# A raw tile for the plain piece and tiles for the unsummed blocks in the first ff's up, in place of a context row and two dot tiles

## The chip, the cores and the metric

The kernel runs on one core of a Trainium2 chip. The metric is the device time of one execution in microseconds (us). The kernel before takes 2824.02 us, the median of 3 runs (2817.88 to 2826.64). The profile is one further execution on the same kind of chip.

## The reference

One layer of a diffusion backbone works on 256 latent tokens and 256 context tokens, 2048 wide, in float32. What matters here:

```
m    = silu(c) @ w_ada + b_ada            # latent: 9 chunks of 2048 (shift, scale, gate for three sub-layers)
m_c  = silu(c_ctx) @ w_ada + b_ada        # context: the same map
h    = rms_norm(s) * (1 + scale) + shift
s    = s + 0.5 * gate * ((silu(h @ w_gate) * (h @ w_up)) @ w_down)     # first ff, 5632 hidden, latent and context
...  token mixing (attention and a long convolution), then a second ff on the latent tokens alone
```

The context is needed only until the mixing's keys and values, so of its modulation only chunks 0 to 4 are used; the latent stream needs all nine.

## The kernel before

Each product is made of three matmuls: a float32 operand is split into a rounded part (`hi`, tile `whi`, a cast on ACT) and a remainder (`lo`, tile `wlo`, a subtraction on DVE), and `mm3` (lines 239 to 241) multiplies hi by hi, hi by lo and lo by hi.

The first ff's up runs over 44 blocks of hidden units, `f1.up(j)`. The first three (`WAVE`) run together in an opening wave. For each later block the 2048 inputs come in four pieces `kq`, each a weight load of 512 KB into a tile `raw` by `weight_load` (line 216, on SP's queue):

- piece 0 is the *plain* one. `prepare` casts it on ACT (L417), negates the cast (L418), and POOL adds the raw weights to it by an accumulating transfer (`u<-raw`, L419). The raw tile is free when the second of these transfers has read it. Piece 0 of block j+1 is prepared after piece 1 of block j.
- pieces 1 to 3 are *summed* from block 9, 7 and 5 on (`QUADS`): a scheme in the manner of Strassen with 14 products of 256 columns in place of 16. `prepare` first splits three of the four 128-wide blocks of the raw tile as they are (the *unsummed* blocks, 128x768: cast L208, subtraction L209), then forms sums in place on DVE (L425, L426, L427), and splits all four (128x1024, L208 and L209 again).

`raw` has four tiles; `whi` and `wlo` have three each, taken in turn by the short and the long splits. After block j PE's banks are combined (L469 to L477) on ACT and DVE, and `keep` (L483 to L487) writes the result to DRAM from ACT and POOL. The summed inputs themselves are made on DVE in the first blocks (`build`).

Beside this, DVE computes modulation chunks 5, 7, 6, 8 (`ADA_UP`) during the up and 2, 3, 4 (`ADA_DOWN`) during the down as dot products: `ada_dve` loads a half row of the transposed map (512 KB, tile `adaw`, four tiles) and multiplies it with a row of silu(c) (`crow0`) and, for chunks below 5, one of silu(c_ctx) (`crow1`), 1.28 us each (L145). `ada_hook` gives out dots after each piece at a rate (`ADA_RATES`: up, and the two passes of the down); `last_load` puts each dot's load behind the weight load traced last on SP's queue. Both rows and the dot tiles lie in the pool `adap`, which is opened after the wave and closed after the down; the rows are loaded by ACT's queue after block 3.

The down (`f1.down`) reads the activations back (POOL, L502) and takes 80 steps of one weight tile each (`weight`: cast L228, subtraction L232) with a call of the hook at each.

A planner orders the instructions of each engine and queue from the program's order and its own estimate of when tiles are free and transfers have landed. At run time every engine and queue goes through its list in that order and waits where something is not there.

## Time and profile before

| what | us |
|---|---|
| median of 3 runs | 2824.02 |
| the profiled execution, its own time | 2818.97 |
| its span, first to last instruction | 2817.2 |
| up with summed pieces, 260 to 1197 | 937.0, PE busy 819.2 |
| down with the dots, 1197 to 1670 | 473.0, PE busy 462.5 |
| the rest, 1670 to 2817 | 1147.0, PE busy 1136.2 |

Times in the profile count from the span's start. A line of a group reads: source line, engine, operation, out<-in by tile name, shapes, count | busy us, mean ns of one | idle time of the engine just before, and what ended it. A line of waits reads: engine, tile and line that waited <- what it waited for: us in total, times, the longest. "PEld" is the weight load of TensorE, "SPq" the DMA queue of SyncE. A busy PE is not PE at its peak, since matmuls overlap and the clock granted to it varies (PEclk, 1.00 is full).

### The profile page before, as it was taken

What the parts mean: (1) busy time and instruction counts of PE and PEld (TensorE: products, weight loads), DVE (VectorE), ACT (ScalarE), POOL (GpSimd) and SP (SyncE); (2) the same over time, 40 slices, a digit from 0 to 9 for tenths busy, and PEclk for the clock granted to TensorE, in tenths of its full rate; (3) what the DMA queues carried; (4) which work ended last, traced back from release to release, by engine and by line L of the source; (5) the groups of instructions that cost most, each with busy time, mean ns of one, the idle gap of its engine ahead of it and who ended that gap; (6) DMA issues with size and microseconds to landing.
All of it is one profiled execution on the core that took longest, in us unless ns stands there. A gap on an engine that the chain in (4) does not pass through costs nothing.

```text
span 2817.2 us, 38140 instructions
## 1 busy us (share of the span) xinstructions
PE 2662.6 (95%) x14480; PEld 2275.9 (81%) x14480; DVE 1910.3 (68%) x3050; ACT 1116.5 (40%) x1545; POOL 253.5 (9%) x394
## 2 busy tenths in 40 slices
PE   8999998988888889899999999999999999999999
PEld 5677888887888878787888798888878888888887
DVE  6756776766776676776898879688875455554444
ACT  5343443434333433321121145546554444444333
POOL 1121111111111111232001100000000000000000
PEclk9999999999999999899999999999999999999999
DMA  9977676767766676899679755634555666666664
GB/s 365 352 232 212 183 214 196 221 196 199 196 200 198 190 209 189 252 393 319 237 261 300 268 189 176 187 112 134 179 170 189 188 191 190 188 191 204 201 202 157
DMA packets 194004, 607.91 MB, mean 216 GB/s; under 512 B 22299, under 2 KB 25308, under 8 KB 189468
## 3 DMA queue, kind: packets, MB, share of 16 engines
q1 hardware_dynamic: 140012, 501.77, 53.7%
q0 software_dynamic: 53184, 100.95, 14.9%
q10 hardware_dynamic: 624, 2.75, 0.3%
q8 instruction: 113, 1.85, 0.3%
q14 instruction: 71, 0.58, 0.1%
HBM read 545.08 MB, written 38.81 MB: 207 GB/s over the span
## 4 chain that ended last, share of the span: by engine, by line
PE 59%; issue 19%; DMA 12%; DVE 6%; POOL 2%; ACT 2%; SPq 0%; POOLq 0%; DVEq 0%; ACTq 0%
PE pa L1254 10%; PE pa L1252 10%; PE pa L1253 9%; DMA adaw<-in_w_adaT_dram 5%; DMA u<-raw 4%; PE pb L241 4%; PE pb L239 4%; PE pb L240 4%; PE pa L247 3%; PE pa L241 3%; PE pa L239 3%; PE pa L240 3%; PE pa L249 2%; DVE adas L145 1%; DMA act<-u 1%
## 5 line engine op out<-in xcount | busy, mean ns | idle before, releaser
L232 DVE TENSOR_TENSOR wlo<-raw,whi 128x1024 fp32r<-128x1024 f32 x487 | 595.5, 1223 | 413.3 <-ACT whi L228 411.5
L228 ACT CAST whi<-raw 128x1024 fp32r<-128x1024 f32 x487 | 512.3, 1052 | 891.6 <-PE pa L1254 413.4
L241 PE MATMUL pa<-u,wlo 128*128 128x256 f32 (+1 forms) x1252 | 416.0, 332 | 36.0 <-DVE wlo L209 29.4
L241 PE MATMUL pb<-u,wlo 128*128 128x256 f32 (+1 forms) x1262 | 412.9, 328 | 37.5 <-DVE wlo L209 30.6
L239 PE MATMUL pa<-u,whi 128*128 128x256 f32 (+1 forms) x1252 | 415.1, 332 | 31.1 <-ACT whi L208 29.0
L239 PE MATMUL pb<-u,whi 128*128 128x256 f32 (+1 forms) x1262 | 412.0, 327 | 25.7 <-ACT whi L208 25.7
L1252 PE MATMUL pa<-whi,u 128*128 128x512 f32 x1060 | 413.9, 391 | 0.0
L1253 PE MATMUL pa<-wlo,u 128*128 128x512 f32 x1060 | 412.8, 390 | 0.2 <-DVE wlo L232 0.2
L1254 PE MATMUL pa<-whi,u 128*128 128x512 f32 x1060 | 412.8, 390 | 0.0
L240 PE MATMUL pa<-u,whi 128*128 128x256 f32 (+1 forms) x1252 | 410.9, 328 | 0.4 <-DVE u L789 0.4
L240 PE MATMUL pb<-u,whi 128*128 128x256 f32 (+1 forms) x1262 | 408.4, 324 | 0.0
L208 ACT CAST whi<-raw 128x768 fp32r<-128x768 f32 x222 | 205.4, 938 | 300.0 <-DVE raw L427 253.1
L145 DVE CUSTOM_DVE_ANT_0 adas<-adaw,crow,mod 128x1024 bf16<-128x1024 f32 x160 | 205.4, 1284 | 162.8 <-DMA adaw<-in_w_adaT_dram 160.8
L209 DVE TENSOR_TENSOR wlo<-raw,whi 128x768 fp32r<-128x768 f32 x222 | 240.2, 1089 | 107.9 <-ACT whi L208 106.9
L241 PEld LDWEIGHTS pb<-u,wlo 128*128 128x128 f32 x1262 | 249.7, 198 | 61.8 <-DVE wlo L209 37.5
L241 PEld LDWEIGHTS pa<-u,wlo 128*128 128x128 f32 x1252 | 249.7, 199 | 61.7 <-DVE wlo L209 35.7
L239 PEld LDWEIGHTS pa<-u,whi 128*128 128x128 f32 x1252 | 249.2, 199 | 57.7 <-ACT whi L208 32.3
L239 PEld LDWEIGHTS pb<-u,whi 128*128 128x128 f32 x1262 | 249.4, 198 | 47.5 <-ACT whi L208 29.2
L145 DVE CUSTOM_DVE_ANT_0 adas<-adaw,crow,cond 128x1024 bf16<-128x1024 f32 x160 | 205.3, 1283 | 112.2 <-DMA adaw<-in_w_adaT_dram 106.0
L240 PEld LDWEIGHTS pa<-u,whi 128*128 128x128 f32 x1252 | 249.3, 199 | 18.5 <-DVE u L789 1.5
L240 PEld LDWEIGHTS pb<-u,whi 128*128 128x128 f32 x1262 | 249.4, 198 | 16.8 <-issue 0.4
L1253 PEld LDWEIGHTS pa<-wlo,u 128*128 128x128 f32 x1060 | 199.1, 188 | 41.5 <-DVE wlo L232 0.6
(337 smaller groups left out, 3652.6 us busy)
## 6 DMA issues: line engine op xcount, KB each, us to landing
adaw<-in_w_adaT_dram SPq DMA_DIRECT2D x223, 512.0 KB, 6.4
raw<-in_w_dn_dram SPq DMA_DIRECT2D x184, 512.0 KB, 3.8
raw<-in_w_up_dram SPq DMA_DIRECT2D x176, 512.0 KB, 3.5
raw<-in_w_up1q_dram SPq DMA_DIRECT2D x164, 512.0 KB, 4.5
u<-act POOLq DMA_DIRECT2D x136, 256.0 KB, 9.0
act<-u POOLq DMA_DIRECT2D x132, 256.0 KB, 2.6
wrow<-in_w_ada_dram SPq DMA_DIRECT2D x32, 1024.0 KB, 9.9
u<-raw POOLq DMA_DIRECT2D x82, 256.0 KB, 6.3
```

The source lines that it names most:

```text
L145: V.tensor_tensor_reduce(out=sc, in0=t, in1=crow[i][:, b * (D // 2) : (b + 1) * (D // 2)], scale=1.0, scalar=mcol if b else bada[:, n : n ...
L208: S.copy(hi, src)
L209: V.tensor_sub(lo, src, hi.bitcast(F32))
L228: S.copy(hi, raw)
L232: V.tensor_sub(lo, raw, hi.bitcast(F32))
L239: PE.matmul(ps, w[0], xx[0], start=start, stop=False)
L240: PE.matmul(ps, w[0], xx[1], start=False, stop=False)
L241: return PE.matmul(ps, w[1], xx[0], start=False, stop=stop)
L247: PE.matmul(ps, w[0], x, start=start, stop=stop)
L1252: PE.matmul(ps[t], hi, w[0], start=start, stop=False)
L1253: PE.matmul(ps[t], hi, w[1], start=False, stop=False)
L1254: last = PE.matmul(ps[t], lo, w[0], start=False, stop=stop)
```

## The change

In the up, `adap` holds one context row (`crow0`) and two dot tiles. The 16 KB per partition given up there hold one raw tile for the plain piece (`plain`, 4 KB; from block 4 on, that is all but the first one prepared) and two tiles each for the rounded and the remainder part of the unsummed blocks (`bhi`, `blo`, 3 KB each). The four `raw` tiles are left to pieces 1 to 3, and the three `whi` and `wlo` to the long splits and to the pieces that aren't summed. The row is loaded ahead of block 3.

After the up the remaining dots of `ADA_UP` are run, `adap` is closed and opened again with both rows, loaded and put through Silu anew, and four dot tiles. The hook starts with a debt of 4, and the rates in the down are 1.15 and 1.42 in place of 1.05 and 1.4.

```
-ADA_RATES = (0.79, 1.05, 1.4)
+ADA_RATES = (0.79, 1.15, 1.42)
 ...
-        t = T(adap, (P, D // 2), "adaw", bufs=4)
+        t = T(adap, (P, D // 2), "adaw", bufs=adaw_bufs)
 ...
-    def weight_load(src, shape, queue=None):
-        raw = T(wp, shape, "raw", bufs=4)
+    def weight_load(src, shape, queue=None, pool=None):
+        raw = T(wp, shape, "raw", bufs=4) if pool is None else T(pool, shape, "plain", bufs=1)
 ...
-            raw = weight_load(self.wupq[j - WAVE, kq], (P, 2, 4, P))
+            pool = adap if kq == 0 and j > WAVE else None
+            raw = weight_load(self.wupq[j - WAVE, kq], (P, 2, 4, P), pool=pool)
 ...
-                hi, lo = T(wp, (P, 2, n, P), "whi", F32R, 3), T(wp, (P, 2, n, P), "wlo", F32R, 3)
+                if n == 3:
+                    hi, lo = (T(adap, (P, 2, n, P), name, F32R, 2) for name in ("bhi", "blo"))
+                else:
+                    hi, lo = (T(wp, (P, 2, n, P), name, F32R, 3) for name in ("whi", "wlo"))
                 out.append(split_to(raw[:, :, 0:n], hi, lo))
 ...
-    adap_cm = tc.tile_pool(name="adap", bufs=2)
-    adap = adap_cm.__enter__()
     crow = []
+
+    def open_dots(n, bufs):
+        nonlocal adap, adap_cm, adaw_bufs
+        adap_cm = tc.tile_pool(name="adap", bufs=2)
+        adap, adaw_bufs = adap_cm.__enter__(), bufs
+        crow.clear()
+        for i in range(n):
+            crow.append(T(adap, (P, D), f"crow{i}", bufs=1))
+            nc.scalar.dma_start(crow[i], a["crow"][i : i + 1, :].partition_broadcast(P))
+            S.activation(crow[i], crow[i], AF.Silu)
+
+    adap = adap_cm = adaw_bufs = None
+    open_dots(1, 2)
 ...
         f1.up(j)
         if j == WAVE:
-            for i in range(2):
-                crow.append(T(adap, (P, D), f"crow{i}", bufs=1))
-                nc.scalar.dma_start(crow[i], a["crow"][i : i + 1, :].partition_broadcast(P))
-                S.activation(crow[i], crow[i], AF.Silu)
             f1.hook = lambda: (next(build, None), ada_hook())
 ...
     norm_plan = iter(NORM_PLAN)
+    while done[0] < len(ADA_UP) * KT * 2:
+        ada_next()
+    adap_cm.__exit__(None, None, None)
+    open_dots(2, 4)
+    owed[0] = -4.0
+
     def down_hook(p):
```

## The prediction

> **What bounds the kernel now.** I read the page first, then the busy times by stage, the waits of the widest gap, and last one stretch of that stage in order of time.
>
> ```profile
> span 2817.2 us, 38140 instructions
> PE 2662.6 (95%) x14480; PEld 2275.9 (81%) x14480; DVE 1910.3 (68%) x3050; ACT 1116.5 (40%) x1545; POOL 253.5 (9%) x394
> ```
>
> PE leaves some 155 us of the span open. The view of windows (PE, weight loads, DVE, ACT, POOL, granted clock, DMA share, GB/s) says where:
>
> ```profile
> core 0: us, PE busy (x) PEld busy (x) DVE busy (x) ACT busy (x) POOL busy (x), PEclk, DMA share, GB/s
> 150.00:260.00 110.00, 105.97 (x503) 88.82 (x502) 64.72 (x112) 47.03 (x70) 21.95 (x30) 0.98 0.80 224
> 260.00:1197.00 937.00, 819.18 (x5470) 763.65 (x5469) 664.01 (x1094) 361.04 (x519) 146.15 (x199) 0.94 0.71 204
> 1197.00:1670.00 473.00, 462.51 (x2120) 383.58 (x2119) 369.45 (x584) 99.79 (x101) 65.44 (x123) 1.00 0.84 287
> 1670.00:2817.00 1147.00, 1136.20 (x5447) 949.25 (x5445) 708.21 (x1015) 542.91 (x736) 0.00 (x0) 1.00 0.57 178
> 843.40:847.20 3.80, 3.04 (x15) 2.84 (x15) 3.48 (x5) 1.07 (x3) 1.77 (x2) 0.56 0.91 115
> 847.40:853.40 6.00, 6.00 (x52) 6.00 (x52) 3.72 (x5) 2.74 (x4) 0.00 (x0) 1.00 0.63 147
> ```
>
> 118 of the 155 us lie in 260 to 1197, the first ff's up with its summed pieces; and there the clock is 0.94, because it is low after each stop (0.56 with 15 matmuls in 3.8 us, then 1.00 with 52 in 6.0). All the rest of the kernel is PE-bound. One hidden block j of that stage takes 25.33 us, by the first and last Silu of 39 ((1198.5 - 235.9) / 38), so the window holds 37 of them:
>
> ```profile
> L476 ACT ACTIVATE sq<-sq x39: 622/632/636, 235.9 to 1198.5; 128x512 f32<-128x512 f32 x39
> ```
>
> What PE would need: three summed pieces of 14 products with 3 matmuls each are 126 matmuls of 256 columns, at 6.0 / 52 = 0.115 us; the plain piece has 24 of 512 columns, at 200 / 901 = 0.222 us by this row of the later ff:
>
> ```profile
> 2150.00:2350.00 200.00, 200.00 (x901) 165.50 (x900) 101.21 (x99) 85.88 (x100) 0.00 (x0) 1.00 0.61 190
> ```
>
> That is 14.5 + 5.3 = 19.8 us, 733 us for 37. So the window could be 204 us shorter if only PE counted. The waits inside the window say who holds it up:
>
> ```profile
> DVE adas L145 <- DMA adaw<-in_w_adaT_dram: 161.9, 59, 6.0
> DVE wlo L209 <- ACT whi L208: 101.1, 90, 2.3
> ...
> PE pb L241 <- DVE wlo L209: 30.6, 25, 4.1
> PE pa L241 <- DVE wlo L209: 29.4, 29, 3.1
> ...
> PE pa L239 <- ACT whi L208: 29.0, 14, 3.2
> ...
> PE pb L239 <- ACT whi L208: 25.7, 17, 3.1
> ```
>
> PE's 118 us are waits for rounded and remainder tiles (114.7 in these four rows). Behind them stands DVE: 664.0 busy + 161.9 for dot tiles + 101.1 for ACT = 927 of 937 us. DVE works through its queue in order and is never idle for want of PE; **DVE's queue is the bound of this stage**, though busy only 71%.
>
> Why the dot tiles are late stands in SP's own waits, and in one block's stretch:
>
> ```profile
> SPq L216 <- DVE wlo L209: 424.7, 58, 11.0
> SPq L216 <- DMA u<-raw: 270.4, 38, 10.5
> ```
> ```profile
> 860.79 9.75 SPq L216 DMA_DIRECT2D raw<-in_w_up1q_dram  x2
> 870.58 0.44 SPq L141 DMA_DIRECT2D adaw<-in_w_adaT_dram  x1
> 879.92 0.80 SPq L216 DMA_DIRECT2D raw<-in_w_up1q_dram  x2
> 880.78 0.90 SPq L141 DMA_DIRECT2D adaw<-in_w_adaT_dram  x2
> ```
> ```profile
> 870.19 1.22 POOL L419 DMA_DIRECT2D u<-raw  x1
> ```
> ```profile
> DMA to landing us min/median/max: 3.3/6.3/9.7
> ```
> ```profile
> 873.99 2.27 DVE L209 TENSOR_TENSOR wlo<-raw,whi 128x1024 fp32r<-128x1024 f32 x2 [1.17 <-ACT whi L208]
> 879.44 1.28 DVE L145 CUSTOM_DVE_ANT_0 adas<-adaw,crow,mod 128x1024 bf16<-128x1024 f32 x1 [3.18 <-DMA adaw<-in_w_adaT_dram]
> ```
>
> Of four raw tiles one is the plain piece's. It is free only when POOL's second accumulating transfer has read it: issued at 870.19, landed 9.7 us later at 879.9 (the maximum of that line's landings), and SP's next raw load leaves at 879.92. That is once per block: 38 waits, 7.1 us each. The raw tile it holds back is a summed piece's, and the dot tiles queue behind it. The dot at 879.44 has its tile from 870.58, 8.9 us earlier.
>
> **The change, part by part.** The sum is made on DVE's 937 us.
>
> *The plain piece's own raw tile, and four raw tiles for three summed pieces.* No summed piece waits for the accumulating transfer any more; it waits for DVE's work four pieces back, more than a block. Of the 59 dot waits I lay 38 to SP's 38 stops, at the mean of 161.9 / 59 = 2.74 us: 104 us. The other 21, 58 us, follow loads that no stop delayed: they are a tile's time to land against where the dot stands in DVE's order, and stay. Bounds for the 104: all gone, or all kept, since the plain load now waits for the same transfer (one tile, last block's accumulation), on SP, with a dot tile and the next raw load queued behind it, and DVE and ACT behind those. One of about three dot tiles per block is traced right behind the plain load, so something remains: I take 20 us, nearer the lower end, since the next raw pieces are then already there and DVE has work to do first. Saved: 84 us.
>
> *Own rounded and remainder tiles (two each) for the three-block part.* The short cast no longer takes turns with the long one in three tiles. DVE's groups in the window:
>
> ```profile
> L209 DVE TENSOR_TENSOR wlo<-raw,whi 128x1024 fp32r<-128x1024 f32 x109 | 133.4, 1223 | 84.9 <-ACT whi L208 84.9
> L209 DVE TENSOR_TENSOR wlo<-raw,whi 128x768 fp32r<-128x768 f32 x108 | 103.2, 955 | 17.2 <-ACT whi L208 16.2
> L145 DVE CUSTOM_DVE_ANT_0 adas<-adaw,crow,mod 128x1024 bf16<-128x1024 f32 x60 | 77.0, 1283 | 84.8 <-DMA adaw<-in_w_adaT_dram 84.6
> ...
> L145 DVE DVE_READ_ACCUMULATOR2_ANT mod<- 128x1 f32 x120 | 10.1, 84 | 0.0
> ```
>
> The 16.2 us before the short subtraction go: they are a cast that was late for a tile or a load. The 84.9 before the long one stay: in-place subtractions, then ACT's cast, then DVE, in series whatever the tiles. Bounds: 0 to 101 saved, the upper if the next piece's short subtraction fills the gap, which the new tiles permit; I take 16. PE also gets more pieces in hand, which helps only if DVE keeps up on the mean.
>
> *Two dot tiles instead of four in the up.* SP's load of a dot now waits for the dot two before it, with the next raw load behind it. 120 dots in 937 us are 7.8 us apart, so a load has 15.6 us:
>
> ```profile
> DMA to landing us min/median/max: 4.4/6.7/11.1
> ```
>
> Even the longest landing of a dot tile fits: nothing. If dots ran in close threes, the third would wait up to 6.7 us; 0 to 20 us in all.
>
> *One context row fewer in the up, loaded before the up.* Dots there use one row. Gone: a broadcast of 1 MB and a Silu of 1.9 us on ACT; the other load keeps its place in ACT's queue at the wave's end. Nothing to -2; I take -2.
>
> ```profile
> u<-act POOLq DMA_DIRECT2D x136, 256.0 KB, 9.0
> ...
> crow<-in_crow_dram ACTq DMA_DIRECT2D x2, 1024.0 KB, 4.5
> ```
> ```profile
> L897 ACT ACTIVATE crow<-crow x2: 1902/1904/1905, 157.2 to 161.5; 128x2048 f32<-128x2048 f32 x2
> ```
>
> *Pool closed and opened again at the down.* The two dots that 160 steps of 0.79 leave (126 of 128) run at the up's end. Then ACT has two loads, which wait for the old tiles' last readers, and two Silus; behind these stand the casts of the down's weights, and PE behind those. Loads of 4.5 to 9.0 us (the latter what transfers take when the down's activations stream in) and 3.8 us of Silu make 12.8 to 21.8 us. Cover for the dots: the debt of 4 means that at 1.15 per step the first comes with the fifth step, and a step is 24 x 0.222 = 5.3 us, so 26.6 us. Cover for PE: the casts run ahead,
>
> ```profile
> ACT whi L228 <- PE pa L240: 186.1, 48, 6.7
> ```
>
> they wait for PE to free one of three tiles, so about two steps, 10.7 us, are in hand. Without all overlap the cost is 21.8 - 10.7 = 11 us; I take 3. Denser dots: 1.42 x 2 x (1.283 + 0.084) + 1.223 = 5.1 us of DVE per step, 5.3 of PE: still covered; before it was 1.4.
>
> The Trainium skill's page "DMA: Bandwidth & Descriptors", section "Queues, rings and completion order", says that each DMA engine takes turns between the queues with work, packet by packet. By that rule the two context rows would share the engines with the weights and the activations and, at a third of the 287 GB/s of the row 1197 to 1670, take some 22 us (an estimate); with the Silus 26 us, the cost 26 - 10.7 = 15 in place of 3, and the total 2737. No row of before shows that load in such traffic.
>
> Sum: DVE's window becomes 937 - 84 - 16 = 837 us, above PE's 733, so DVE stays the bound. With -2 and +3 the change is -99. The profiled execution's own time is 2818.97 us (span 2817.2, 1.8 around it), so 2720; the median of the runs lies 5.05 above that execution. **Forecast: 2725 us.**
>
> **The rivals.**
> *PE becomes the bound:* all dot waits and half of ACT's go, DVE needs 664 + 50 + 10 = 724, less than PE's 733. With a few stops left, 770: gain 167, 2657 us. For it: deeper tiles let DVE fill gaps. Against: in-order DVE at 724 of 733 leaves no slack.
> *It does not do what it says:* SP keeps its order, plain load ahead of the next summed piece, so these still leave when the accumulation lands. The 270 us of SP stops remain, only the 16.2 and a few waits of PE go: gain 10 to 45, about 2795. For it: the stops are SP's, and the plain load's source of delay, 3.3 to 9.7 us, is untouched. Against: four tiles let the summed load go earlier.
> *Slower:* the stop moves onto the plain load, and the dot tile behind it becomes the late one. Before, plain load and its dot tile left at 870.2 and 870.58, freed by DVE; now they would leave at 879.9, 9.7 us later, the tile landing at about 880.3 + 6.7 = 887.0 instead of 879.4. If DVE's order keeps the dot where it stands, each block pays 7.6 and saves 2.74: +4.9 x 37 = +180, near 3000. It decides when DVE reaches that dot less than 4.9 us later in its work than now; half way it is +90, 2914.
>
> **How the numbers follow.** Forecast with its neighbourhood (gain 45 to 150): 0.56. PE bound: 0.13. Little done: 0.14, most of it still over 0.3% faster (0.3% is about what can be told from no change here, 8 us). Slower: 0.13. No change: 0.04. The range, 2665 to 2815, holds the forecast, the little-done case and the upper part of PE bound: 0.8 together. Its ends are gains of 159 (just short of where PE binds) and of 10 (only the late short casts gone, less the down's cost). Faster 0.81, same 0.06, slower 0.13.
>
> **What would show it.** In 260 us to the up's end: about 22.6 us between Silus; DVE's waits for dot tiles from 161.9 down to about 80 with fewer than 40 stops; the long subtraction still waiting some 85 on ACT; SP's waits for the accumulation now before plain loads alone; clock up from 0.94. Wrong if DVE's waits for dot tiles stay above 140, if PE's busy share in the stage passes 97%, or if the down's first 100 us grow by over 15.

## The result and the profile after

The changed kernel takes 2807.73 us (median of 7 runs, 2801.81 to 2812.43) against 2823.61 us (7 runs, 2816.01 to 2826.64): a ratio of 0.995 with a 95% interval of 0.9934 to 0.9965. It is some 16 us faster; the forecast was 99. The profiled execution took 2812.43 us, the longest of its seven, 6.5 us less than the one before; the traces can account for these 6.5 us only.

The page of the changed kernel, its span and its first engine line:

```profile
span 2810.7 us, 37981 instructions
PE 2653.9 (94%) x14480; PEld 2255.6 (80%) x14480; DVE 1914.2 (68%) x3050; ACT 1112.7 (40%) x1546; POOL 253.5 (9%) x394
```

Where the 6.5 us come from is read from three lines of code. The copy of a bank by ACT (L469 before, L473 after) runs once in each block of the first ff's up, so its last start is the up's end; the first matmul of the projection to keys and values (L965, L982) is the down's end. Each row gives count, shortest, median and longest duration in ns, first and last start. Before:

```profile
L469 ACT COPY sq<-pb x20: 362/374/377, 226.4 to 1194.0; 128x256 f32<-128x256 f32 x20
L965 PE MATMUL pa<-whi,u x128: 387/389/628, 1690.7 to 1927.1; 128*128 128x512 f32 x128
```

After, with the Silu of the blocks (L480):

```profile
L473 ACT COPY sq<-pb x20: 358/363/374, 236.5 to 1163.8; 128x256 f32<-128x256 f32 x20
L480 ACT ACTIVATE sq<-sq x39: 620/631/634, 242.6 to 1166.6; 128x512 f32<-128x512 f32 x39
L982 PE MATMUL pa<-whi,u x128: 387/389/629, 1682.8 to 1919.2; 128*128 128x512 f32 x128
```

The up ends 30.2 us earlier (1163.8 against 1194.0). The stretch from there to the projection grows by 22.3 us, from 496.7 to 519.0. A block takes 24.32 us ((1166.6 - 242.6) / 38) in place of 25.33; the prediction expected 22.6.

Of the 30.2 us, 10.7 come in the last block alone. PE begins its products at 1162.39 before and at 1142.88 after, 19.5 us earlier:

```profile
1162.39 0.40 PE L239 MATMUL pb<-u,u 128*128 128x512 f32 x1
```
```profile
1142.88 0.40 PE L239 MATMUL pb<-u,u 128*128 128x512 f32 x1
```

So this block takes 31.6 us to its bank copy before and 20.9 us after. Before, seven dot instructions (L145) start between the last two bank copies and 132 by the up's end; in the changed kernel none and 128, since the next dots wait for the second opening. A part of what the up gains there is work that comes later.

**The up.** The waits in 260 to 1197 (total, times, longest, in us). The window is that of the prediction and here includes 33 us of the down, so its totals are, if anything, a little high for the up:

```profile
DVE adas L145 <- DMA adaw<-in_w_adaT_dram: 156.5, 51, 7.9
...
DVE wlo L209 <- ACT whi L208: 65.6, 60, 1.2
...
PE pa L239 <- ACT whi L208: 21.5, 15, 5.7
PE pa L241 <- DVE wlo L209: 20.6, 21, 2.3
...
PE pb L239 <- ACT whi L208: 17.1, 13, 4.3
...
PE pb L241 <- DVE wlo L209: 14.5, 20, 1.4
...
DVE blo L209 <- ACT bhi L208: 13.6, 14, 2.6
```

PE's waits in these rows fell from 114.7 to 73.7 us, and DVE's waits for ACT from 101.1 to 79.2 (65.6 + 13.6). Its waits for dot tiles, from which 84 us were to come, are 156.5 against 161.9. SP's own waits in the same window show that its stops did not go, they changed place:

```profile
SPq L216 <- DVE wlo L209: 399.3, 81, 9.9
SPq L216 <- DMA u<-plain: 157.2, 36, 8.2
SPq L141 <- DMA adaw<-in_w_adaT_dram: 139.7, 41, 5.8
```

The stop on the accumulation is now at the plain piece's own load (`u<-plain`, 36 times), and a second kind has come: SP waits at a dot tile's load (L141) for an earlier dot that itself waits for its transfer. Before, the stops on the accumulation summed to 270.4; now the two rows sum to 296.9. One block in order of time, what SP issued (start, us, line, transfer, number):

```profile
723.60 0.33 SPq L216 DMA_DIRECT2D plain<-in_w_up1q_dram  x1
723.98 0.90 SPq L141 DMA_DIRECT2D adaw<-in_w_adaT_dram  x2
724.98 0.38 SPq L216 DMA_DIRECT2D raw<-in_w_up1q_dram  x1
730.72 0.33 SPq L141 DMA_DIRECT2D adaw<-in_w_adaT_dram  x1
```

and what DVE did then:

```profile
724.80 0.41 DVE L474 TENSOR_TENSOR mt<-sq,pb 128x256 f32<-128x256 f32 x1
729.40 1.29 DVE L145 CUSTOM_DVE_ANT_0 adas<-adaw,crow,cond 128x1024 bf16<-128x1024 f32 x1 [4.19 <-DMA adaw<-in_w_adaT_dram]
...
731.61 0.42 DVE L428 TENSOR_TENSOR raw<-raw 128x256 f32<-128x256 f32 x1
```

The plain load leaves when the last block's accumulation has landed. Right behind it stand two dot tiles. DVE is at the first of these dots at 725.2 and gets the tile at 729.4; the in-place subtraction L428 of a summed piece, and with it ACT's cast and PE's next products, stands behind that dot. The third dot tile of the block has to wait until this dot is done (730.72), with SP's next raw load behind it. Counted in SP's loads in order of time, 27 of the 33 plain loads between 260 and 1070 are followed directly by two dot tiles.

**The down.** PE's first 20 us after the up's end: before, then after, by the view of windows (PE, weight loads, DVE, ACT, POOL, granted clock, DMA share, GB/s):

```profile
1194.00:1214.00 20.00, 20.00 (x88) 16.58 (x88) 18.09 (x30) 6.36 (x8) 5.69 (x10) 0.96 1.09 393
```
```profile
1164.00:1184.00 20.00, 6.57 (x16) 3.10 (x15) 8.50 (x14) 6.61 (x7) 7.25 (x13) 0.64 1.08 388
```

72 matmuls fewer at the 4.4 per us of the first row are 16 us of the 22. The waits from 1155 to 1220 of the changed kernel say for what:

```profile
PE pa L239 <- DMA u<-act: 9.3, 2, 8.5
...
DVE adas L145 <- ACT crow L897: 8.9, 1, 8.9
```

PE waits for the down's activations, and then runs at a clock of 0.64. Their first fetch by POOL left 17.7 us before the up's end in the kernel before (1176.3 against 1194.0), 7.5 us in the changed one (1156.3 against 1163.8):

```profile
L502 POOL DMA_DIRECT2D u<-act x136: 527/536/906, 1176.3 to 1579.1; - x136
```
```profile
L506 POOL DMA_DIRECT2D u<-act x136: 527/535/917, 1156.3 to 1567.6; - x136
```

These fetches stand in POOL's queue behind the stores of the last block but one. POOL waited for that block's result in the kernel before as well; before, then after:

```profile
1175.14 0.56 POOL L485 DMA_DIRECT2D act<-u  x1 [20.15 <-ACT u L483]
```
```profile
1155.71 0.56 POOL L489 DMA_DIRECT2D act<-u  x1 [17.69 <-ACT u L487]
```

So POOL's wait isn't new: its store leaves 19.4 us earlier, as PE comes to the last block 19.5 us earlier. The fetch is late because the last block, which covers it, is 10.7 us shorter.

### The profile page after: what moved, and what is told of

Read it like the earlier page. It is cut to its first block, busy times and chain, and to the rows that moved or that the text cites. A ratio compares the mean times of both kernels' runs of the same rounds, so it can differ in the third digit from the quotient of the medians.

```text
span 2810.7 us, 37981 instructions
## 1 busy us (share of the span) xinstructions
PE 2653.9 (94%) x14480; PEld 2255.6 (80%) x14480; DVE 1914.2 (68%) x3050; ACT 1112.7 (40%) x1546; POOL 253.5 (9%) x394
## 4 chain that ended last, share of the span: by engine, by line
PE 53%; issue 22%; DMA 14%; DVE 7%; POOL 3%; ACT 1%; SPq 0%; POOLq 0%; DVEq 0%; ACTq 0%
PE pa L1270 9%; PE pa L1271 9%; PE pa L1269 9%; DMA adaw<-in_w_adaT_dram 6%; PE pa L247 3%; DMA act<-u 3%; PE pb L241 3%; PE pb L239 3%; PE pb L240 3%; DVE adas L145 2%; PE pa L239 2%; PE pa L240 2%; PE pa L241 2%; DMA u<-plain 2%; PE pa L249 2%
## 5 line engine op out<-in xcount | busy, mean ns | idle before, releaser
L228 ACT CAST whi<-raw 128x1024 fp32r<-128x1024 f32 x487 | 511.9, 1052 | 882.9 <-PE pa L1271 413.4
L239 PE MATMUL pa<-u,whi 128*128 128x256 f32 (+1 forms) x928 | 318.3, 344 | 32.9 <-ACT whi L208 21.5
L241 PE MATMUL pa<-u,wlo 128*128 128x256 f32 (+1 forms) x928 | 316.2, 341 | 24.1 <-DVE wlo L209 20.6
L241 PE MATMUL pb<-u,wlo 128*128 128x256 f32 (+1 forms) x920 | 310.8, 338 | 23.1 <-DVE wlo L209 14.5
L239 PE MATMUL pb<-u,whi 128*128 128x256 f32 (+1 forms) x920 | 311.2, 338 | 17.2 <-ACT whi L208 17.1
L240 PE MATMUL pa<-u,whi 128*128 128x256 f32 (+1 forms) x928 | 314.2, 339 | 4.5 <-DMA u<-act 4.1
L240 PE MATMUL pb<-u,whi 128*128 128x256 f32 (+1 forms) x920 | 307.7, 334 | 0.0
L145 DVE CUSTOM_DVE_ANT_0 adas<-adaw,crow,mod 128x1024 bf16<-128x1024 f32 x160 | 205.2, 1283 | 130.7 <-DMA adaw<-in_w_adaT_dram 128.3
L145 DVE CUSTOM_DVE_ANT_0 adas<-adaw,crow,cond 128x1024 bf16<-128x1024 f32 x160 | 205.1, 1282 | 127.2 <-DMA adaw<-in_w_adaT_dram 116.4
L208 ACT CAST whi<-raw 128x1024 fp32r<-128x1024 f32 x111 | 116.3, 1048 | 430.5 <-DVE raw L428 430.5
L1269 PEld LDWEIGHTS pa<-whi,u 128*128 128x128 f32 x1060 | 199.0, 188 | 41.7 <-ACT whi L228 1.1
L1271 PEld LDWEIGHTS pa<-whi,u 128*128 128x128 f32 x1060 | 199.0, 188 | 41.3
L239 PEld LDWEIGHTS pa<-u,whi 128*128 128x128 f32 x928 | 180.1, 194 | 60.2 <-ACT whi L208 24.6
L241 PEld LDWEIGHTS pa<-u,wlo 128*128 128x128 f32 x928 | 180.5, 195 | 47.4 <-DVE wlo L209 25.5
L241 PEld LDWEIGHTS pb<-u,wlo 128*128 128x128 f32 x920 | 179.0, 195 | 46.6 <-DVE wlo L209 19.3
L239 PEld LDWEIGHTS pb<-u,whi 128*128 128x128 f32 x920 | 178.9, 194 | 37.8 <-ACT whi L208 20.2
L240 PEld LDWEIGHTS pa<-u,whi 128*128 128x128 f32 x928 | 180.5, 195 | 23.4 <-DMA u<-act 5.7
```

The lines of the kernel that those rows point to most:

```text
L145: V.tensor_tensor_reduce(out=sc, in0=t, in1=crow[i][:, b * (D // 2) : (b + 1) * (D // 2)], scale=1.0, scalar=mcol if b else bada[:, n : n ...
L208: S.copy(hi, src)
L228: S.copy(hi, raw)
L239: PE.matmul(ps, w[0], xx[0], start=start, stop=False)
L240: PE.matmul(ps, w[0], xx[1], start=False, stop=False)
L241: return PE.matmul(ps, w[1], xx[0], start=False, stop=stop)
```

## The experiments

All ratios are to the kernel before, run on the same chip, with 95% intervals; "per block" is the mean distance of the Silus, "down" the stretch from the last bank copy to the projection, from each kernel's trace. The ring is the ring `u` of 58 tiles; rows that say so have fewer.

| kernel | us | ratio | per block | down |
|---|---|---|---|---|
| changed kernel | 2807.73 | 0.995 (0.9934 to 0.9965) | 24.32 | 519.0 |
| dots not behind plain | 2745.46 | 0.9734 (0.9714 to 0.9755) | 22.83 | 512.5 |
| before, dots not behind plain | 2794.62 | 0.9906 (0.9884 to 0.9928) | 24.51 | 498.6 |
| plain tile alone | 2837.0 | 1.006 (1.0038 to 1.0082) | 25.78 | 504.8 |
| plain tile, dots not behind it | 2791.49 | 0.9892 (0.9875 to 0.9908) | 24.57 | 511.1 |
| blocks' tiles alone | 2788.15 | 0.988 (0.9852 to 0.9909) | 23.77 | 518.8 |
| blocks' tiles, dots not behind plain | 2795.89 | 0.9911 (0.9896 to 0.9926) | 24.02 | 517.0 |
| two plain tiles, ring of 56 | 2798.44 | 0.9919 (0.9897 to 0.9941) | 24.00 | 514.3 |
| changed, one dot tile loaded once | 2657.14 | 0.9421 (0.9391 to 0.945) | 20.58 | 515.7 |
| before, one dot tile loaded once | 2720.73 | 0.9646 (0.9617 to 0.9676) | 22.86 | 499.1 |
| changed, three dot tiles, ring of 56 | 2777.7 | 0.9845 (0.9829 to 0.9862) | 23.62 | 511.6 |
| before, two dot tiles | 2821.27 | 1.0 (0.999 to 1.0009) | 25.41 | 496.2 |
| changed, rows not reloaded | 2796.07 | 0.9911 (0.9886 to 0.9936) | 24.19 | 516.2 |
| not behind plain, earlier fetch | 2740.85 | 0.9715 (0.9698 to 0.9731) | 22.85 | 508.4 |
| the same, three dot tiles, ring of 56 | 2710.43 | 0.9606 (0.959 to 0.9622) | 22.12 | 506.9 |
| the same, four dot tiles, ring of 54 | 2794.98 | 0.9916 (0.9898 to 0.9933) | 24.27 | 509.2 |
| the same, three dot tiles, ring of 54 | 2794.9 | 0.9903 (0.9875 to 0.9931) | 24.43 | 508.4 |
| not behind plain, rows later | 2747.71 | 0.9743 (0.9726 to 0.976) | 23.04 | 516.1 |
| not behind plain, rows later, earlier fetch | 2745.97 | 0.9735 (0.9714 to 0.9756) | 22.88 | 507.9 |

In "plain tile, dots not behind it" the last Silu comes 18.8 us after the last bank copy (4.5 before), so its 24.57 is some 0.3 too high; by the bank copies it is 24.29.

### Are the dots late because they stand behind the plain load?

`weight_load` notes its last load, and the dots' loads are issued after the noted one. The edit leaves the plain load out of the note:

```
-        if done[0]:
+        if done[0] and pool is None:
             last_load[0] = load
```

> The kernel after, but a dot tile's load is placed behind the latest load of a summed piece and no longer behind the plain piece's load. Theory (the stop has moved): SP stops at the plain load until the accumulation has landed, two dot tiles stand behind it, and DVE waits for them. Then DVE's waits for dot tiles in 260 to 1197 fall from 156.5 us to about 60, a block goes from 24.3 to about 22.3 us, and the whole falls by some 70 us to about 2735. Rival (DVE's chain is the bound whatever is late): the wait moves to another instruction, a block stays at 23.8 us or more and the whole within 15 us of 2808.

62 us faster than the changed kernel; the theory's 70 us and 22.3 us per block are nearly reached, its 60 us of dot waits are not. SP's waits in 260 to 1130 of this kernel:

```profile
SPq L216 <- DMA u<-plain: 379.4, 43, 13.2
SPq L216 <- DVE wlo L209: 280.3, 70, 13.4
SPq L141 <- DVE mod L145: 35.3, 27, 2.0
```

DVE's wait for dot tiles there:

```profile
DVE adas L145 <- DMA adaw<-in_w_adaT_dram: 105.2, 60, 5.6
```

And one block of SP:

```profile
716.21 0.33 SPq L216 DMA_DIRECT2D plain<-in_w_up1q_dram  x1
716.59 0.42 SPq L216 DMA_DIRECT2D raw<-in_w_up1q_dram  x1
717.11 0.38 SPq L141 DMA_DIRECT2D adaw<-in_w_adaT_dram  x1
719.21 0.33 SPq L216 DMA_DIRECT2D raw<-in_w_up1q_dram  x1
719.63 0.38 SPq L141 DMA_DIRECT2D adaw<-in_w_adaT_dram  x1
```

SP still stands at the plain load, and longer than in the changed kernel (379.4 us against 157.2). But behind the plain load a raw piece follows first: 32 of the 35 plain loads between 260 and 1070 have one right behind them, and none has two dot tiles. So the length of SP's stops is not what cost the time; the edit changed what stands behind them.

The same edit on the kernel before (the plain load marked by a flag, all else as before):

> The kernel before with only the other edit of the last experiment: a dot tile's load is not placed behind the plain piece's load. Theory (in before the load that stops on the accumulation is a summed piece's, and one dot tile per block follows that one whatever the plain load does): the whole stays within 15 us of before. Rival (the placing of the dots alone gives the gain, and the new tiles nothing): a gain of 50 us or more, about 2760 or less.

It gives 27 us, between the two expectations: the place of the dots costs the kernel before something as well, but less than half of the 62 us that it costs the changed one.

A second tile for the plain piece, for two of the 58 tiles of the ring `u`:

```
-... T(pool, shape, "plain", bufs=1)      -... T(up, shape, "u", dt, 58)
+... T(pool, shape, "plain", bufs=2)      +... T(up, shape, "u", dt, 56)
```

> The kernel after with two raw tiles for the plain piece (and 56 in place of 58 of the 2 KB work tiles, which make the room). The dots stay behind the plain load, but that load no longer stops SP until the accumulation of the block before has landed. Theory (the stop is what keeps the dots late): DVE's waits for dot tiles fall from 156.5 us in 260 to 1197 to 110 or less, SP's stops on the accumulation go below 40 us, a block is at 23 us or less, the whole about 2750. Rival (being behind the plain load in the queue is enough to be late, stop or no stop): within 15 us of 2808.

9 us faster, DVE's dot waits 147.0 us. But the trace shows SP still waiting for `u<-plain` 37 times, 356.9 us in 260 to 1130: with two tiles the plain load is placed a block earlier in SP's queue and meets the accumulation there. Right behind it stands one dot tile (17 of 33 times) or a raw piece. So this run did not take the stop away, and can't say whether the stop or the place in the queue makes the dots late; the ring is two tiles shorter too.

### The parts alone, and what they are worth together

The plain piece's tile without the unsummed blocks' tiles:

```
-                if n == 3:
+                if False:
                     hi, lo = (T(adap, (P, 2, n, P), name, F32R, 2) for name in ("bhi", "blo"))
```

> The kernel after without the tiles for the unsummed blocks (short and long splits take turns in three tiles again); the plain piece keeps its own raw tile. If the plain tile does the work of the change: about after, 2800 to 2815. If the block tiles do: 2820 to 2845, as before plus the down's loss of 22 us.

The blocks' tiles without the plain piece's:

```
-            pool = adap if kq == 0 and j > WAVE else None
+            pool = None
```

> The kernel after without the plain piece's own raw tile (four raw tiles for all four pieces); the unsummed blocks keep their own tiles. If the block tiles do the work of the change: 2800 to 2820. If the plain tile does: 2825 to 2850, since SP's stop is again before a summed piece and the dots have two tiles.

The split of the forecast gain, 84 to 16, was the wrong way round. Plain's tile alone makes the kernel slower by 0.6%; the blocks' tiles alone gain 1.2%, more than both together. Both kernels have the rest of the change (one row, two dot tiles, the second opening). DVE's dot waits in 260 to 1130, a window that lies inside the up of all four kernels: before, with plain's tile alone, with the blocks' tiles alone, and with both:

```profile
DVE adas L145 <- DMA adaw<-in_w_adaT_dram: 145.6, 54, 6.0
```
```profile
DVE adas L145 <- DMA adaw<-in_w_adaT_dram: 186.4, 47, 7.8
```
```profile
DVE adas L145 <- DMA adaw<-in_w_adaT_dram: 91.7, 60, 5.5
```
```profile
DVE adas L145 <- DMA adaw<-in_w_adaT_dram: 151.5, 49, 7.9
```

Plain's own tile adds to the waits that it was to take away, with the blocks' tiles and without; it is the blocks' tiles that shorten them. The two remaining corners, each part with the dots not behind the plain load:

> The changed kernel with the plain piece back in the four shared raw tiles (as in the kernel with the unsummed blocks' tiles alone, 2788.15 us, 23.77 us per block), and the dots' loads no longer placed behind the plain load. It asks what the plain piece's own tile is worth once the dots don't stand behind it: the kernel with both and that edit takes 2745.46 us and 22.83 per block. Theory (its own tile pays as soon as the dots are out of its way): 2760 to 2780 us, 23.2 to 23.6 per block, so the own tile is worth 15 to 35 us there, after having cost some 20 in the change as made. Rival (own tile worth nothing, the unsummed blocks' tiles and the dots' places give all): within 8 us of 2745, 22.7 to 23.0 per block.

> The changed kernel without the unsummed blocks' own tiles (as in the kernel with the plain piece's tile alone, 2837.0 us, 25.78 us per block), and the dots' loads no longer placed behind the plain load. It is the last corner of a cube of three edits: plain's own tile, blocks' tiles, dots not behind the plain load. The kernel before takes 2823.6, with the dots' edit alone 2794.6, with plain's tile alone 2837.0, with the blocks' tiles alone 2788.2, with the blocks' tiles and the dots' edit 2795.9, with all three 2745.5. Theory (plain's own tile pays wherever the dots are out of its way, whatever the other tiles): 2740 to 2780 us, 23.0 to 24.4 per block. Rival (its gain needs the blocks' tiles too, since without them ACT and DVE have nowhere to put the pieces that arrive early): 2785 to 2800, no better than the dots' edit alone.

The median, and in brackets the up's end in the profiled execution, both in us:

| | dots behind plain | dots not behind plain |
|---|---|---|
| neither part | 2823.6 (1194.0) | 2794.6 (1164.4) |
| plain's tile | 2837.0 (1205.0) | 2791.5 (1149.9) |
| blocks' tiles | 2788.2 (1141.9) | 2795.9 (1150.5) |
| both | 2807.7 (1163.8) | 2745.5 (1102.2) |

The first row has one opening of the pool and four dot tiles, so a step down from it also holds the rest of the change, above all a down that is 8 to 22 us longer. The up's ends leave the down out. By them plain's own tile costs 11 and 22 us with the dots behind it; with the dots' edit it gains 14.5 us without the blocks' tiles and 48 with them. By the medians the gain is 50 us with the blocks' tiles (the expectation was 15 to 35) and 3 without, where the longer down takes the rest; so the expectation that it pays "whatever the other tiles" failed for the whole.

Why it gains so much less without the blocks' tiles no run separates. One reason stands in the trace: the edit did not do its work there. In that kernel 18 of the 33 plain loads between 260 and 1070 still have a dot tile's load right behind them, against 3 of 35 with the blocks' tiles, and DVE waits 137.9 us for dot tiles in 260 to 1130, against 105.2.

### What the dot loads cost at all

In both kernels the dots of the up read one tile that is loaded once; 127 loads are left out, and the modulation chunks computed there are not the layer's. The core of the edit:

```
+        if c >= 5 and once:
+            t = once[0]          # the tile of the first dot, no load
```

> The kernel after, but all dots of the up read one tile that is loaded once, so that 127 loads of 512 KB are left out there and the modulation it computes is not the layer's; DVE's instructions are the same. It prices the dot tiles' loads as a whole. Theory: DVE has 676 us of work and 79 us of waits for ACT in the window of 937, so a block falls to about 20.5 to 21.5 us and the up by 105 to 140 us. Rival: other waits fill in, a block stays above 23 us.

> The kernel before with the same edit: dots of the up read one tile that is loaded once (the modulation is not the layer's). SP's stops for the accumulation then hold back summed pieces alone. Theory: DVE's 162 us of dot waits turn partly into ACT's waits for raw tiles: a block about 23 us against 25.3. If the dot tiles alone are what DVE waits for: about 21. If the late summed pieces alone cost the time: 25 as before.

The dots' transfers, with all that waits for them, cost the changed kernel 150 us and the one before 100. In the one before a block falls to 22.86 us, the 23 of its theory: there neither the dot tiles alone (21) nor the late summed pieces alone (25) make the time. Without the transfers the changed kernel's up is bound by PE, from 260 to its end at 1016:

```profile
260.00:1016.00 756.00, 752.17 (x5446) 714.98 (x5445) 615.80 (x1024) 355.95 (x513) 143.08 (x194) 1.00 0.62 166
```

PE is busy 752 of 756 us at a clock of 1.00, 20.6 us per block. The change is worth 64 us there (2720.73 to 2657.14), and 79 us by the up's end (1094.8 to 1015.9).

### Two dot tiles, three, four

The changed kernel with three dot tiles in the up, again for two tiles of the ring:

```
-    open_dots(1, 2)        -        return T(up, shape, "u", dt, 58)
+    open_dots(1, 3)        +        return T(up, shape, "u", dt, 56)
```

> The changed kernel with three dot tiles in the up in place of two (paid for with two of the 58 tiles of the ring u). The prediction held two tiles to cost nothing, 0 to 20 us at most. In the changed kernel SP stands 139.7 us (41 times) at a dot tile's load in the window. Theory (the dots are late because two of them stand behind the plain load, the number of tiles is not the limit): 2798 to 2812 us, dot waits of DVE still above 130 us in 260 to 1130. Rival (SP's stops at dot tiles are the two tiles' own price, and hold up the raw loads behind them): 2770 us or less, SP's waits at dot loads gone, DVE's dot waits below 100.

30 us faster. DVE's wait in 260 to 1070 in the changed kernel, and with the third tile:

```profile
DVE adas L145 <- DMA adaw<-in_w_adaT_dram: 143.5, 46, 7.9
```
```profile
DVE adas L145 <- DMA adaw<-in_w_adaT_dram: 97.3, 39, 5.9
```

SP's stops at dot loads in that window went from 123.1 to 22.0 us (35 to 5 times). The rival is nearer: two tiles are a limit here. In the kernel before, however, where `ada_dve` takes two tiles in the up in place of four (the down keeps four):

```
-        t = T(adap, (P, D // 2), "adaw", bufs=4)
+        t = T(adap, (P, D // 2), "adaw" if c >= 5 or b else "adaw2", bufs=2)
```

> The kernel before with two dot tiles in the up in place of four, and nothing else (the down keeps four, in two pairs). It measures by itself the edit that the prediction held to cost nothing. Theory (two tiles cost this stage some 30 us, as the third tile gained 30 in the changed kernel and 30 in the best one): 2845 to 2870 us, 26.0 to 26.7 us per block in place of 25.33, SP's waits at dot loads up from 23.3 us. Rival (two tiles cost only where the dots stand behind the plain piece's own tile; before, each load has time): within 8 us of 2822.

it costs nothing: 1.0 (0.999 to 1.0009), though SP now stands 54.7 us at dot loads in 260 to 1197, where the kernel before has no such row (the expectation's 23.3 us is in none of its views). So two tiles have a price only together with another part of the change, and SP's stops at dot loads are not that price by themselves.

On the kernel with the dots apart from the plain load and the earlier fetch of the next section, a third tile, a fourth one, and a run that takes away only the ring tiles that the fourth was paid with (`open_dots(1, 3)` and a ring of 56; `open_dots(1, 4)` and 54; `open_dots(1, 3)` and 54):

> The kernel with the dots out from behind the plain load and the activations fetched earlier (2740.85 us; 22.85 us per block), with three dot tiles in the up in place of two. Leaving 127 of the 128 dot loads out took the changed kernel to 20.6 us per block, so dot waits still cost this one about 2 us per block. Theory (two tiles cost nothing: the landing of a tile against the dot's place in DVE's order decides): within 6 us of 2741, 22.6 to 23.0 per block. Rival (a third tile lets loads leave a dot earlier): 2700 to 2725 us, 21.5 to 22.3 per block, DVE's dot waits from 105 to below 70 us in 260 to 1130.

> The best kernel so far (2710.43 us, three dot tiles, 22.12 us per block), with a fourth dot tile for two more tiles of the ring u. Theory (each tile lets a load leave one dot earlier, and DVE's dot waits, 73.3 us in 260 to 1070, go further): 2690 to 2703 us, 21.5 to 21.9 per block. Rival (the third tile took all that tiles can take, the rest is the raw loads' and the casts' doing, and the ring u becomes short: ACT's minus-cast already waits 76.0 us for activations stored from that ring): 2705 to 2725 us.

> The kernel with three dot tiles (2710.43 us, ring u of 56 tiles), with two tiles of the ring u fewer (54) and nothing in their place. The kernel with four dot tiles and 54 tiles took 2794.98 us; in it ACT's minus-cast of the plain piece waited 219.1 us in 260 to 1070 for results that were still being stored from the ring, and PE 33.1 us for the accumulation of the plain piece. Theory (the ring of 54 is too short, the number of dot tiles is not what cost 84 us): 2770 to 2800 us, the same two waits. Rival (a fourth dot tile changes the order in which the loads are placed, and that cost the time): 2705 to 2725 us.

The third tile gains 30 us: 2710.43 us, 4% less than before, the fastest kernel here that computes the layer. It gains them where hardly a stop at dot loads was left to take away (8.3 us in 260 to 1070, then 0.9) and no plain load has two dot tiles behind it; DVE's dot waits there fall from 98.6 to 73.3 us. Why a third tile is worth 30 us in these two kernels and two tiles cost nothing in the one before stays open. With a ring of 54 it takes 2794.9 with three tiles and 2794.98 with four, so the ring is what cost 84 us. Waits in 260 to 1070 with three tiles and a ring of 54:

```profile
ACT u L419 <- DMA act<-u: 221.5, 62, 6.6
...
DVE adas L145 <- DMA adaw<-in_w_adaT_dram: 43.3, 39, 2.5
PE pb L241 <- DMA u<-plain: 39.1, 15, 4.3
```

and with a ring of 56:

```profile
ACT u L419 <- DMA act<-u: 76.0, 28, 5.9
DVE adas L145 <- DMA adaw<-in_w_adaT_dram: 73.3, 54, 5.8
```

The negated cast of the plain piece writes into the ring and waits for a result of the block before to be stored from there; with 54 tiles PE then waits for the plain piece itself. DVE's dot waits are lower in the slower kernel: a sum of waits is no measure of what they cost when another engine has become the bound.

### Where the down's 22 us went

The second opening of the pool without the two rows' load and Silu (a constant in their place, so chunks 2 to 4 are not the layer's):

```
+            if n == 2:
+                G.memset(crow[i], 1.0)
+                continue
             nc.scalar.dma_start(crow[i], a["crow"][i : i + 1, :].partition_broadcast(P))
```

> The kernel after, but the two context rows of the second opening are not loaded nor put through Silu: POOL fills them with ones (chunks 2 to 4 of the modulation are then not the layer's). The up is as after. Theory (the rows' 2 MB among the activations' transfers delay these): PE's wait of 8.9 us for activations at the down's start shrinks below 3, ACT's 9 us of waiting and Silu go, and the whole is 10 to 16 us below after. Rival (the up's end comes sooner after the activations are first asked for, 7.5 us against 17.6): PE still waits 8 us or more and the whole falls by less than 5.

The down falls by 2.8 us only, and PE's wait for the activations (L239) stays, 8.9 us against 9.3. POOL writes the constant, and DVE's first dot waits 14.5 us for it, longer than for the rows, so the run prices the rows' loads and Silus and not that wait. The whole fell by 11.7 us; in the profiled executions 6.2 of 10.4 us lie in the up, which the edit does not touch, and are not the rows' price. So on the kernel with the dots out of the way the fetch was put earlier, the rows later, and both:

```
-                if j == JT - 1 and kq < 2:
+                if (j, kq) in ((JT - 2, 3), (JT - 1, 1)):
                     for n in range(GRP):
-                        self.fetch(ORDERS[0], kq, n)
+                        self.fetch(ORDERS[0], int(j == JT - 1), n)
```

> The kernel in which the dots no longer stand behind the plain load (2745.46 us; down 512.5 us from the up's last bank copy to the first KV projection), and the down's first four activation fetches are issued one to two pieces of block 43 or 42 earlier. In the ten kernels run so far the lead of the first fetch before the up's last bank copy and the length of the down go together: leads of 16.2 to 18.3 us with downs of 496.8 to 504.8, leads of 7.5 to 12.0 with downs of 512.5 to 519.0. Theory (the late fetch makes the larger part of the down's loss): the first fetch leads by over 17 us, PE's waits for activations at the start of the down (4.1 and 3.9 us) go, the down takes 500 to 506 us, the total is 2732 to 2740. Rival (the loss is the reopening: rows, dot tiles and denser dots, and the short lead only goes along with it): the down stays at 510 or more, the total within 5 us of 2745, or above it because the fetch takes tiles and POOL's time from the up's last blocks.

```
-ADA_RATES = (0.79, 1.15, 1.42)
+ADA_RATES = (0.79, 1.28, 1.42)
 ...
-    open_dots(2, 4)
-    owed[0] = -4.0
     def down_hook(p):
+        steps_done[0] += 1
+        if steps_done[0] < 5:
+            return
+        if steps_done[0] == 5:
+            with tc.issue_after(cast[0].ins):      # the step's last cast
+                open_dots(2, 4)
+            owed[0] = -4.0
```

> The same kernel (2745.46 us), with the dots' tiles and the two context rows opened at the down's fifth step behind that step's cast, and a rate of 1.28 dots per step in place of 1.15 in the first pass. The fetches of the activations stay. Theory (late fetch): the down gains 2 to 6 us, what the reopening costs in the kernel that has the plain piece's tile alone (504.8 against 496.8, with a lead of 16.2 us against 17.7); total 2739 to 2744. Rival (the reopening's burst at the boundary): the down falls to 500 to 503, total 2733 to 2736.

> Both edits of the two kernels before this one together. Theory: the two causes add, the down is back at the 497 to 500 us of the kernel before, total 2728 to 2734. If the late fetch alone matters, it equals the kernel with the earlier fetch within 3 us; if the burst alone matters, the kernel with the later rows.

The first 20 us of the down with the earlier fetch, then with both edits:

```profile
1105.00:1125.00 20.00, 16.33 (x64) 12.46 (x63) 11.79 (x17) 8.31 (x8) 4.28 (x8) 0.91 1.08 385
```
```profile
1104.00:1124.00 20.00, 20.00 (x91) 16.59 (x90) 7.14 (x12) 8.02 (x9) 3.21 (x6) 1.00 1.05 377
```

With the earlier fetch PE no longer waits for activations; one cast that stands behind a row's Silu costs it 3.6 us, and the down falls from 512.5 to 508.4, short of the 500 to 506 expected. With the later rows alone it grows, to 516.1. With both, PE starts as in the kernel before (91 matmuls against 88), yet the down takes 507.9. The waits of that kernel in 1104 to 1220 show the loss further on:

```profile
DVE adas L145 <- ACT crow L897: 10.5, 2, 7.3
...
PE pb L241 <- DVE wlo L232: 9.4, 5, 4.2
```

DVE now waits for the rows with a dot, the weights' remainders stand behind the dot, and PE waits for these. Opening the rows later moved their cost. No variant with the pool opened twice came below 504.8 us (plain's tile alone, where the fetch leads the up's end by 16.2 us), against 496.2 to 499.1 in the four with one pool. So the 22 us have no single cause. In the changed kernel 16 of them are missing at the entrance, where the wait that ends last is the fetch's, with the low clock that follows. But an earlier fetch was not run on that kernel; on the one with the dots out of the way it gave back 4 us of the 16 by which its down is longer than before, since other waits then end last. And the kernel with plain's tile alone, whose fetch is not late, still has a down 8 us longer: so much belongs to the second opening and the denser dots. The rows' loads and Silus are some 3; the rest was not separated. The totals of the three variants, 2740.85 to 2747.71, are too close to 2745.46 to rank them by time.

## Why the prediction was wrong, point by point

- **"DVE's queue is the bound of this stage"** held. In 260 to 1197 of the changed kernel DVE is busy for 675.9 us and waits 156.5 for dot tiles, 79.2 for ACT and 20.2 at the down's start, 932 of 937 us in all. With the dots' loads left out PE binds at 20.6 us per block; the prediction's count of PE's work was 19.8.
- **"No summed piece waits for the accumulating transfer any more ... Saved: 84 us"** failed; it is the step that broke the forecast. Plain's own tile, as the change has it, saves no dot wait: alone it takes them from 145.6 to 186.4 us, with the blocks' tiles from 91.7 to 151.5 (260 to 1130), and the up ends 11 and 22 us later for it. The prediction wrote that one of about three dot tiles is traced right behind the plain load, and priced what remains at 20 us, "since the next raw pieces are then already there and DVE has work to do first". In the changed kernel two dot tiles stand behind it (27 times of 33), and DVE reaches the first some 4 us too soon. With that one condition lifted the kernel takes 2745.46 us.
- **"The 16.2 us before the short subtraction go ... The 84.9 before the long one stay"**: the amount was near, 22 us, the place was not. Long and short were to keep 84.9 and 0; they have 65.6 and 13.6. The part's worth by itself is larger: 35 us (2788.15), forecast 16, within the bounds of 0 to 101; the up alone ends 52 us earlier with it. And it works in another way than forecast: its kernel waits more for ACT, not less, and 54 us less for dot tiles.
- **"Two dot tiles instead of four ... nothing"**: true of the order that it was read from (1.0 in the kernel before) and false of the order that the change makes (30 us, above the bound of 20). The reckoning with 7.8 us between dots took an even spacing; the trace of the changed kernel has two in a row and a third that waits for the first. That is not the whole of it, since the third tile is worth as much where the dots are spread.
- **Pool opened again, "I take 3"**: measured 22 us. The rows' loads and Silus, on which the cost was worked out, are some 3 of it. At the entrance, where 16 are missing, PE waits for a transfer that the prediction did not look at: the activations' fetch stands in POOL's queue behind the stores of the last block but one, and the last block, which covers it, takes 20.9 us in place of 31.6. The fetch is a part of the loss and not all of it: 8 us came where it was not late.
- By the Trainium skill's page "DMA: Bandwidth & Descriptors", section "Queues, rings and completion order", the prediction estimated 22 us for the rows among other queues' traffic. The trace doesn't bear out that size: the two loads at the down left at 1161.3 and 1163.8, and the second row's Silu began at 1174.9, 13.6 us after the first left. The three row loads of the kernel took (shortest, median, longest):

```profile
DMA to landing us min/median/max: 5.7/8.7/11.1
```

- **The rivals.** The outcome lies nearest to "It does not do what it says" (2795), though for another reason in part: its 270 us of stops did remain, as 296.9, with nearly half of them new ones at dot loads. The mechanism of "Slower", the stop on the plain load with the dot behind it late, is what the trace shows, at 4.2 and 5.1 us in the two blocks read, and plain's tile alone is slower by it. The two were written as alternatives; they act together, and the blocks' tiles pay for them. "PE becomes the bound" came true only without the dots' loads (2657.14; that the rival said 2657 is chance, since that kernel leaves out 127 loads and has the longer down).
- Of the signs that would make it wrong, two came: dot waits above 140, and the down's start longer by over 15.

With the dots off the plain load, the earlier fetch and three dot tiles, 2710.43 us lie below the forecast of 2725, but with three more edits, one of which gives the kernel before 27 us without any of the change's tiles. With the dots off the plain load in both, the change is worth 49 us (2794.62 to 2745.46), half of what was forecast.

## What to carry to other kernels

When a stop is to be taken from a queue, write down the queue's new order and see what stands behind the stop's new place: SP's stops grew here in the kernel that gained 62 us, and what counted was which transfers stood behind them and how soon they were wanted. A part's worth, measured alone, can have another sign than in company (plain's tile moves the up's end by +11, +22, -14.5, -48 us), so a sum over parts is no forecast where they share a queue. And when a stage gets shorter, look at what the next stage must have ready at its start: that transfer's lead shrinks with the stage.

## What the runs showed that was not expected

- Two of 56 tiles of a ring, taken away, cost 84 us, while the two before them, from 58 to 56, could be given for a dot tile at a gain of 30 us. What those first two cost by themselves was not run.
- The clock was low where PE had stopped: it is 0.64 in the 20 us at the down's start in which PE waited for activations, and 1.00 in a whole stage of 756 us in which PE stopped for under 4 us.
- A second tile for the plain piece did not shorten SP's stop on its accumulation (356.9 us against 157.2 with one tile), because the load then stood a block earlier in the queue.
